# A list-scheduled encoder layer: new costs for the first loads and the shared port, sums moved behind the merges, one more Strassen pair

## The chip, the cores and the metric

The kernel runs on one core of one Trainium2 chip. The metric is the device time of one execution in microseconds. Engines are named as in the profile: PE (TensorE, matmuls and transposes), DVE (VectorE), ACT (ScalarE), POOL (GpSimd), SP (SyncE, which issues every DMA of this kernel).

## What is computed

One encoder layer is applied to a prompt of 512 tokens and to a sample of 1024 tokens, with the same weights and a model width of 1024. In the reference, shortened:

```python
h = rmsnorm(x, norm_g)
qa, ka, va, za, qb, kb, vb, zb, ga, gb = split(h @ w_in)
oa = (neighbourhood_attention(rmsnorm(qa), rmsnorm(ka), va, rpb_a) * silu(za)) @ w_o_a   # branch A, 8 heads
ob = (window_gqa_attention(rmsnorm(qb), rmsnorm(kb), vb, t5, sink) * silu(zb)) @ w_o_b   # branch B, 8 heads, 2 for k and v
merged = sigmoid(ga) * oa + sigmoid(gb) * ob
return x + merged @ w_out
```

All data is float32. The kernel multiplies at nearly that precision: every operand is split into a high part (`hi`, rounded by a copy on ACT) and a low part (`lo = x - hi`, a subtraction on DVE or POOL), and each product is three matmuls, hi*hi, hi*lo and lo*hi.

## The kernel before

**Who decides the order.** The program is written as a list of operations (`Flow.op`), each with the engines that may run it, a cost in ns for each, a priority (small is first), and the tiles it writes and reads. `Flow.run` is a list scheduler: it plays the operations through with those costs, gives every engine its next operation by priority, and writes the instructions in the order so found. On the chip each engine then works through its own fixed list and waits at semaphores; nothing is reordered there. SP's list of DMAs is made in the same way (`Flow.dma`: 470 ns on SP, then `nbytes / 360` ns of transfer), so a DMA that waits holds up every later one.

Three of the scheduler's rules matter here. A tag in `IN_TURN` gets its buffers in the order in which the program names the tiles. `port=True` marks an operation for which POOL and DVE exclude each other: while one of the two runs a marked operation, `barred` keeps marked operations off the other. Without a mark given, only operations that either engine may run are marked.

**Stages.** Prompt first (`attention_phase`, then `dense_phase`), then the sample, with the sample's normalisation hidden inside the prompt's phases.

- *Start*: x is loaded in tiles of 128 tokens (`norm_tile`). For the first tile ACT squares and sums (line 460), POOL makes 1/rms (464, 468), DVE multiplies by it and by the gains (line 520, four pieces of 256 columns; the gains row was spread over the partitions by PE at line 1629 and is copied to SBUF by ACT at line 1641), PE transposes (532), ACT and DVE split into `hh` and `hl` (537, 542). The first weights are split by ACT (line 602, `whi`) and POOL or DVE (line 607, `wlo`); `FIRST_POOL` sends the first one to POOL alone.
- *Attention*: for six groups (branch A 0 to 3, branch B 0 and 1) and each token tile, 24 matmuls of 384 columns (`project`, line 761), q and k normalised (785 to 816), transposed (`make_qk`, line 861) and split (882 to 901), scores (line 934), softmax (969 to 1010), transposes of the weights (1026), the product with v (1063). Branch B first gathers every 4th or 8th token column of `hh` and `hl` into `hb` (lines 662 and 664).
- *Dense*: projections z and the gates g, then the merges (for each of eight row blocks m: two products with w_o, times the gate, added, and split back into `hh`/`hl`, which are overwritten), then the projection with w_out. The last products are made in pairs of 128-row blocks, either classically (`pair_classic`: 4 banks of 24 matmuls for the sample) or by one step of Strassen's scheme (`pair_strassen`: 7 products of 12 matmuls). `CLASSIC_S` says how many z, g and w_out pairs of the sample are classic, `CLASSIC_P` the same for the prompt.

**The sums.** A Strassen pair needs four sums of blocks of the right-hand side. For w_out these are made by `sums`: for each k of 4, ten additions on DVE or POOL (line 1161, into three rotating `S` tiles) and four splits into `T` tiles (1167 on ACT, 1172 on DVE or POOL). The eight `T` buffers are held by the gated branch outputs until the merges' last products have read them. In the order before, all of this has priority 20, that of the first w_out pair; the merges have 12 to 19.

## Time and profile before

| what | value |
|---|---|
| three runs | 1144.78, 1145.87, 1147.69 us; median 1145.87 us |
| the profiled execution | 1146.52 us |
| its span, first to last instruction | 1144.7 us (1.8 us lie around it) |
| PE busy | 1133.8 us, 99% of the span |
| DVE, ACT, POOL busy | 854.4, 644.9, 308.3 us |
| merges of the sample end, w_out begins | 1059.7 us |

A PE matmul is recorded from its issue to its end and overlaps the next, so a mean of 389 ns is not what one costs: matmuls that follow each other start some 0.23 us apart at 512 columns. Idle time of PE is therefore looked for in the waits, not in the busy share.

### The profile page before, as it was taken

To read this page: it belongs to the slowest core of one execution; us is meant where nothing else is said; L and a number is where in the kernel's file an instruction comes from. 1 tells how busy PE (TensorE), PEld (TensorE's weight loads), DVE (VectorE), ACT (ScalarE), POOL (GpSimd) and SP (SyncE) were. 2 spreads that over 40 slices of the span, in tenths; PEclk is the share of its full clock that TensorE was granted. 3 is DMA by queue.
4 is the path that set the end of the run, shared out by engine and by line. 5 is a ranking of instruction groups with operands and counts; after the bars stand their busy time and mean duration, and the time that the engine had idled before them with its cause. 6 is when DMAs were issued, how large, how long until landed. Compare 5 with 4: busy or idle time off the path is not lost.

```text
span 1144.7 us, 18482 instructions
## 1 busy us (share of the span) xinstructions
PE 1133.8 (99%) x6139; PEld 985.8 (86%) x6139; DVE 854.4 (75%) x1975; ACT 644.9 (56%) x1467; POOL 308.3 (27%) x413
## 2 busy tenths in 40 slices
PE   8999999999999999999999999999999999999998
PEld 6999988888888899999999888888888888788887
DVE  5888798497765468887778888865878755497984
ACT  5777987544433346665678988865534434343320
POOL 3653433000010054343333445330222210132110
PEclk9999999999999999999999999999999999999999
DMA  7854543488786422121221213226657335573072
GB/s 253 273 158 141 181 113 102 115 264 266 232 277 199 165 72 67 25 70 32 71 61 50 56 37 93 56 66 214 218 148 211 129 111 159 200 238 121 29 223 90
DMA packets 124705, 159.86 MB, mean 140 GB/s; under 512 B 28297, under 2 KB 66961, under 8 KB 124610
## 3 DMA queue, kind: packets, MB, share of 16 engines
q1 hardware_dynamic: 124610, 158.69, 45.4%
q8 instruction: 48, 0.79, 0.3%
q14 instruction: 47, 0.39, 0.1%
HBM read 121.93 MB, written 41.44 MB: 143 GB/s over the span
## 4 chain that ended last, share of the span: by engine, by line
PE 94%; DVE 2%; DMA 2%; ACT 1%; POOL 1%; issue 0%; SPq 0%; ACTq 0%; POOLq 0%
PE p L761 25%; PE x L1285 9%; PE x L1286 9%; PE x L1284 9%; PE x L1063 5%; PE x L1026 5%; PE x L934 4%; PE p L1284 4%; PE p L1285 4%; PE d L1284 4%; PE p L1286 4%; PE d L1286 4%; PE d L1285 4%; PE x L861 2%; DMA ot<-u_d 1%; DMA w<-in_w_att_dram 1%
## 5 line engine op out<-in xcount | busy, mean ns | idle before, releaser
L761 PE MATMUL p<-whi,hh 128*128 128x384 f32 x384 | 133.4, 348 | 0.0
L761 PE MATMUL p<-wlo,hh 128*128 128x384 f32 x384 | 133.1, 347 | 0.0
L761 PE MATMUL p<-whi,hl 128*128 128x384 f32 x384 | 132.4, 345 | 0.0
L978 ACT ACTIVATE sb<-sb,mx 128x384 f32<-128x384 f32 (+1 forms) x192 | 107.5, 563 | 22.4 <-DVE mx L969 22.2
L1167 ACT ACTIVATE whi<-raw 128x512 fp32r<-128x512 f32 (+1 forms) x140 | 81.1, 590 | 52.6 <-PE x L1285 26.2
L761 PE MATMUL p<-whi,hb 128*128 128x384 f32 x384 | 107.5, 347 | 0.0
L1172 POOL TENSOR_TENSOR wlo<-raw,whi 128x512 fp32r<-128x512 f32 (+1 forms) x29 | 40.9, 1413 | 242.4 <-ACT whi L1167 130.4
L1284 PE MATMUL x<-hh,whi 128*128 128x512 f32 x264 | 102.7, 389 | 0.0
L1285 PE MATMUL x<-hl,whi 128*128 128x512 f32 x264 | 102.7, 389 | 0.0
L1286 PE MATMUL x<-hh,wlo 128*128 128x512 f32 x264 | 102.7, 389 | 0.0
L1037 DVE TENSOR_TENSOR pp<-x,pp 128x512 fp32r<-128x512 f32 (+1 forms) x136 | 82.6, 638 | 18.9 <-ACT pp L1032 17.8
L1172 DVE TENSOR_TENSOR wlo<-raw,whi 128x512 fp32r<-128x512 f32 (+1 forms) x111 | 70.1, 645 | 30.5 <-ACT whi L1167 30.2
L1285 PE MATMUL x<-T,whi 128*128 128x512 f32 x224 | 87.5, 390 | 0.3 <-DVE T L1172 0.2
L1286 PE MATMUL x<-T,wlo 128*128 128x512 f32 x224 | 87.2, 389 | 0.0
L1284 PE MATMUL x<-T,whi 128*128 128x512 f32 x224 | 87.1, 389 | 0.0
L1032 ACT ACTIVATE pp<-x 128x512 fp32r<-128x512 f32 (+1 forms) x136 | 70.9, 560 | 22.8 <-PE x L1026 21.8
L799 POOL TENSOR_TENSOR rs_r<-rs_v,mhalf 128x4 f32<-128x4 f32 (+1 forms) x72 | 81.7, 1134 | 5.7
L1063 PE MATMUL x<-pp,v 128*128 128x256 f32 (+1 forms) x368 | 77.8, 324 | 0.8 <-DVE pp L1037 0.8
L792 POOL TENSOR_SCALAR rs_v<-ss 128x4 f32<-128x4 f32 (+1 forms) x72 | 26.2, 364 | 187.3 <-DVE ss L785 184.6
L761 PEld LDWEIGHTS p<-whi,hl 128*128 128x128 f32 x384 | 73.0, 190 | 1.3 <-issue 1.0
L761 PEld LDWEIGHTS p<-wlo,hh 128*128 128x128 f32 x384 | 73.0, 190 | 1.0 <-issue 0.5
L761 PEld LDWEIGHTS p<-whi,hh 128*128 128x128 f32 x384 | 73.0, 190 | 0.9 <-issue 0.5
(351 smaller groups left out, 2985.5 us busy)
## 6 DMA issues: line engine op xcount, KB each, us to landing
raw<-in_w_g_dram SPq DMA_DIRECT2D x76, 256.0 KB
w<-in_w_att_dram SPq DMA_DIRECT2D x46, 384.0 KB
ot<-o_d SPq DMA_DIRECT2D x36, 256.0 KB
g_d<-C SPq DMA_DIRECT2D x34, 256.0 KB
raw<-in_w_z_dram SPq DMA_DIRECT2D x32, 256.0 KB
raw<-in_w_out_dram SPq DMA_DIRECT2D x32, 256.0 KB
C<-g_d SPq DMA_DIRECT2D x24, 256.0 KB
out_dram<-C SPq DMA_DIRECT2D x23, 256.0 KB
```

Of the source, the lines that this page charges most:

```text
L761: pe.matmul(ps.t[:, :GW], part[u](k), mv.t[:, c], start=k == 0 and m == 0, stop=k == KC - 1 and m == 2,)
L799: lambda e: nc.gpsimd.tensor_tensor(r.t[:, :nn], rv.t[:, :nn], mhalf[:, :nn], op=ALU.pow),
L978: act.activation(sb.t[:, :width], sb.t[:, :width], AF.Exp, bias=mx.t[:, i : i + 1], scale=-1.0, accum_out=sm.t[:, i : i + 1],)
L1026: pe.transpose(pt.t[:, u * P : (u + 1) * P], sbs[i].t[:, c * P : (c + 1) * P], ident)
L1032: lambda e, pt=pt, pp=pp, nn=nn: act.activation(pp.t[:, 0, :nn], pt.t[:, :nn], AF.Copy),
L1037: lambda e, pt=pt, pp=pp, nn=nn: dve.tensor_tensor(pp.t[:, 1, :nn], pt.t[:, :nn], pp.t[:, 0, :nn].bitcast(F32), op=ALU.subtract),
L1063: pe.matmul(out(), v.t[:, vs], mv(), start=first, stop=last)
L1167: (("act", ACT_(n)),), lambda e: act.activation(hi(), src(), AF.Copy), prio,
L1172: lambda e: engines[e].tensor_tensor(lo(), src(), hi().bitcast(F32), op=ALU.subtract), prio,
L1284: pe.matmul(out, hi.t[:, cs], mh(), start=first and k == 0, stop=False)
L1285: pe.matmul(out, hi.t[:, cs], ml(), start=False, stop=False)
L1286: pe.matmul(out, lo.t[:, cs], mh(), start=False, stop=last and k == len(ws) - 1)
```

## The change

- `dma`: transfers with a scheduled priority under -2, the first loads, are counted at 230 bytes per ns, not 360; the scheduler counts PE at 1.85 times its cost while its own clock is under 13000 ns.
- `att_weights`: the low part is marked `port=True` for every choice of engines, the one on POOL alone included.
- Costs: `make_qk`'s two DVE operations 105 ns less each, branch B's bias copy on ACT 76 ns more, the gather into `hb` on ACT 1000 ns, before 960.
- `hb` joins `IN_TURN`.
- `sums` for w_out takes a priority for each k (19.2 to 19.5, right behind the merges). For k = 0, 1, 2 the sums are stored to DRAM (`to_d`, 12 stores of 256 KB); later they are loaded back into `U` tiles (12 loads) and split from there at priority 20. For k = 3 they are split from `S` as before. The splits are now in the order in which Strassen uses them (j = 1, 2, 0, 3).
- `CLASSIC_S` ends in 1, not 2: one of the two classic w_out pairs of the sample becomes a Strassen pair.
- `SEED`, `SPREAD`, `SPAN`: with `SPREAD = 0` they shift no priority.

```diff
-CLASSIC_S = (1, 0, 2)
+CLASSIC_S = (1, 0, 1)
+SEED, SPREAD, SPAN, COLD = 0, 0, 1, 13000
+EARLY_RATE = 230
...
-    IN_TURN = {"whi", "wlo", "w32", "T", "S", "raw", "U", "C", "ot"}
+    IN_TURN = {"whi", "wlo", "w32", "T", "S", "raw", "U", "C", "ot", "hb"}
...
-        return self.op((("sp", 470),), lambda e: emit(), prio, lag=nbytes / 360, **kw)
+        return self.op((("sp", 470),), lambda e: emit(), prio, lag=nbytes / (EARLY_RATE if prio < -2 else 360), **kw)
...
-                        ns = dict(o.choice)[e]
+                        ns = dict(o.choice)[e] * (1.85 if e == "pe" and now < COLD and o.prio > -20.5 else 1)
...
-            tuple((e, {"pool": POOL_, "dve": DVE_}[e](n)) for e in engs), emit, prio, new=[lo], use=[hi], hold=[st], after=[a],
+            tuple((e, {"pool": POOL_, "dve": DVE_}[e](n)) for e in engs), emit, prio, new=[lo], use=[hi], hold=[st], after=[a], port=True,
...
-                    f.op((("act", ACT_(GW)),), emit, prio, new=first, use=[raw], into=[nb_t])
+                    f.op((("act", ACT_(GW) + 76),), emit, prio, new=first, use=[raw], into=[nb_t])
...
-                            (("act", 960), ("dve", DVE_(512))),
+                            (("act", 1000), ("dve", DVE_(512))),
...
-                (("dve", DVE_(P) + 165),),
+                (("dve", DVE_(P) + 60),),
...
-                (("dve", DVE_(n) + 165),),
+                (("dve", DVE_(n) + 60),),
...
-        def sums(prio, done):
+        def sums(split_prio, done, prios=None):
...
+                prio = prios[k] if prios else split_prio
...
                 for j in (0, 2, 1, 3):
-                    vh, vl = tv[j]
-                    ops[j, k] = split(
-                        lambda vh=vh, k=k: vh.t[:, k], lambda vl=vl, k=k: vl.t[:, k], lambda v=t[j]: v.t[:, :sn], sn, prio,
-                        (vh, k == 0), (vl, k == 0), [t[j]],
+                    if prios and k < 3:
+                        away.append((j, k, dma(
+                            lambda j=j, k=k, v=t[j]: nc.sync.dma_start(to_d[j, k], v.t[:, :sn]), 512 * sn, prio, use=[t[j]]
+                        )))
+                    else:
+                        away.append((j, k, t[j]))
+            for j, k, v in sorted(away, key=lambda a: ((1, 2, 0, 3).index(a[0]), a[1])) if prios else away:
+                vh, vl = tv[j]
+                if prios and k < 3:
+                    o, v = v, tile_("U", 4)
+                    dma(
+                        lambda j=j, k=k, v=v: nc.sync.dma_start(v.t[:, :sn], to_d[j, k]), 512 * sn, split_prio, new=[v],
+                        after=[o],
                     )
+                ops[j, k] = split(
+                    lambda vh=vh, k=k: vh.t[:, k], lambda vl=vl, k=k: vl.t[:, k], lambda v=v: v.t[:, :sn], sn, split_prio,
+                    (vh, j not in firsts), (vl, j not in firsts), [v],
+                )
+                firsts[j] = True
...
-        mov_h, mov_t = blocks(m_ops, nh), sums(20, m_ops) if o_classic < 4 else None
+        mov_h, mov_t = blocks(m_ops, nh), sums(20, m_ops, [19.2 + 0.1 * k for k in range(4)]) if o_classic < 4 else None
```

The prompt's w_out pairs are all classic, so `sums` with priorities is met in the sample alone. Counted over the whole program, PE has 12 matmuls of 512 columns less (6124 for 6136), SP 24 DMAs more, and DVE, ACT and POOL 5, 7 and 10 instructions more. The line numbers of the changed kernel are 4 larger up to the attention phase and 5 to 21 larger behind it (520 becomes 524, 607 becomes 611, 1161 becomes 1166, 1172 becomes 1177).

**The start, DVE.** `xt` is the first token tile, `x` a PSUM bank, `w_123` and `w_125` the second weight load, `bias` the tile that holds the third and fourth. Before:

```order
L520 SCALAR_TENSOR_TENSOR xt<-xt,nr,x 128x256 x2
L607 TENSOR_TENSOR wlo<-w_123,whi 128x768
L520 SCALAR_TENSOR_TENSOR xt<-xt,nr,x 128x256 x2
L542 TENSOR_TENSOR hl<-x,hh 128x2x128 x3
L520 SCALAR_TENSOR_TENSOR xt<-xt,nr,rb 128x512
L607 TENSOR_TENSOR wlo<-bias,whi 128x768
L542 TENSOR_TENSOR hl<-x,hh 128x2x128
```

Now:

```order
L524 SCALAR_TENSOR_TENSOR xt<-xt,nr,x 128x256 x4
L546 TENSOR_TENSOR hl<-x,hh 128x2x128 x2
L611 TENSOR_TENSOR wlo<-w_125,whi 128x768
L546 TENSOR_TENSOR hl<-x,hh 128x2x128 x2
L524 SCALAR_TENSOR_TENSOR xt<-xt,nr,rb 128x512
L611 TENSOR_TENSOR wlo<-bias,whi 128x768
L524 SCALAR_TENSOR_TENSOR xt<-xt,nr,rb 128x512
```

The low part of the second weights stood between the two halves of the first tile's multiplication; all four pieces now come first, and that low part stands behind two `hl` splits.

**The start, ACT.** `junk` is the square and sum of a token tile, the second one that of tile 1. Before:

```order
L460 ACTIVATE junk,ns<-xt 128x1024
L602 ACTIVATE whi<-w_121 128x768
L602 ACTIVATE whi<-w_123 128x768
L1641 ACTIVATE rb<-x 128x512
L460 ACTIVATE junk,ns<-xt 128x1024
L537 ACTIVATE hh<-x 128x2x128 x3
L602 ACTIVATE whi<-bias 128x768
```

Now:

```order
L464 ACTIVATE junk,ns<-xt 128x1024
L606 ACTIVATE whi<-w_123 128x768
L1662 ACTIVATE rb<-x 128x512
L606 ACTIVATE whi<-w_125 128x768
L541 ACTIVATE hh<-x 128x2x128 x2
L1662 ACTIVATE rb<-x 128x512
L541 ACTIVATE hh<-x 128x2x128 x2
L464 ACTIVATE junk,ns<-xt 128x1024
```

Tile 1's square stood ahead of tile 0's splits into `hh`; it now stands behind all four.

**The w_out projection of the sample, DVE.** Buffer numbers are kept. `hl_3331` and `hl_3377` are the low part of the merged activations, `d_`, `p_` and `x_` PSUM banks, `raw_` loaded weights, `S_` sums (of weights or activations). Before, from the last splits of the sums to the first Strassen weights:

```order
L1172 TENSOR_TENSOR T_12820<-S_13005,T_12811 128x512
L1161 TENSOR_TENSOR S_13025<-S_13025,hl_3331 128x512
L1161 TENSOR_TENSOR C_12680<-x_12822,C_12680 128x512
L1161 TENSOR_TENSOR C_12716<-x_12868,C_12716 128x512
L1161 TENSOR_TENSOR C_12764<-x_12910,C_12764 128x512
L1161 TENSOR_TENSOR C_12813<-x_12951,C_12813 128x512
L1172 TENSOR_TENSOR wlo_13051<-raw_12726,whi_12893 128x512
L1172 TENSOR_TENSOR wlo_13057<-raw_12747,whi_12917 128x512
L1172 TENSOR_TENSOR wlo_13066<-raw_12826,whi_12973 128x512
L1161 TENSOR_TENSOR C_12860<-d_12992,C_12860 128x512
L1161 TENSOR_TENSOR S_13094<-raw_13044,raw_13059 128x512
L1161 TENSOR_TENSOR C_13064<-p_13012,C_13064 128x512
```

Now, from the last splits of the sums on:

```order
L1166 TENSOR_TENSOR S_13050<-raw_12696,raw_12768 128x512
L1177 TENSOR_TENSOR T_13042<-U_13010,T_13026 128x512
L1177 TENSOR_TENSOR T_13042<-U_13022,T_13026 128x512
L1177 TENSOR_TENSOR T_13042<-S_13031,T_13026 128x512
L1166 TENSOR_TENSOR C_12842<-x_12997,C_12842 128x512
L1166 TENSOR_TENSOR S_13082<-raw_12667,raw_12696 128x512
L1166 TENSOR_TENSOR C_12880<-C_12880,U_13076 128x512
L1177 TENSOR_TENSOR wlo_13024<-S_13070,whi_12974 128x512
L1177 TENSOR_TENSOR wlo_13102<-S_13082,whi_13091 128x512
L1177 TENSOR_TENSOR wlo_13111<-S_13050,whi_13099 128x256
L1177 TENSOR_TENSOR wlo_13102<-S_13050,whi_13091 128x256
L1177 TENSOR_TENSOR wlo_13111<-raw_12768,whi_13099 128x512
```

Before, the first of these posts, `C_12680<-x_12822`, came 44 rows behind the last merge bank's addition (`U_12666<-x_12793`), and on PE the first product with a sum stood 216 matmuls behind the merges' last: two classic pairs and two products of the first Strassen pair. Now it stands 120 matmuls behind: one classic pair and two products. The low part of that product's weights, `wlo_13024<-S_13070`, comes 39 rows behind `U_12683<-x_12822`, the last merge bank's addition, and right behind `C_12880<-C_12880,U_13076`, where `U_13076` is ACT's copy of the first Strassen product's bank, `d_13052`.

**The w_out projection of the sample, SP.** `C` tiles are loaded from x and stored as output, `to_d` holds the sums. Before, from the merges' last loads on:

```order
L1249 DMA raw_12647<-in_w_out_dram 128x512
L1563 DMA U_12666<-g_d1024_94 128x512
L1249 DMA raw_12672<-in_w_out_dram 128x512
L1443 DMA C_12680<-in_xt_s_dram 128x512
L1443 DMA C_12716<-in_xt_s_dram 128x512
L1249 DMA raw_12726<-in_w_out_dram 128x512
L1249 DMA raw_12747<-in_w_out_dram 128x512
L1443 DMA C_12764<-in_xt_s_dram 128x512
L1443 DMA C_12813<-in_xt_s_dram 128x512
```

Now, at the same place, behind the merges' last loads:

```order
L1238 DMA U_12788<-to_d1024_95 128x512
L1464 DMA C_12795<-in_xt_s_dram 128x512
L1229 DMA to_d1024_95<-S_12773 128x512
L1229 DMA to_d1024_95<-S_12780 128x512
L1464 DMA C_12842<-in_xt_s_dram 128x512
L1229 DMA to_d1024_95<-S_12807 128x512
L1229 DMA to_d1024_95<-S_12848 128x512
L1464 DMA C_12880<-in_xt_s_dram 128x512
L1238 DMA U_12892<-to_d1024_95 128x512
L1229 DMA to_d1024_95<-S_12878 128x512
L1238 DMA U_12904<-to_d1024_95 128x512
```

Stores of sums and loads of them now stand between the loads of x and of the weights.

More of the change, by code (lines that the diff above doesn't have):

```diff
@@ L169, in op @@
         o.key, o.outs, o.eng = len(self.ops), [], None
+        if self.slack != 1:
+            o.prio += SPREAD * (hash((SEED, o.key // SPAN)) % 1000 / 1000 - 0.5)
         o.port = {"dve", "pool"} <= {e for e, _ in choice} if port is None else port
@@ L1146, in dense_phase @@
         u_d = dpool.tile([8, P, nt], F32, tag=f"u_d{nt}", name=f"u_d{nt}")
+        to_d = dpool.tile([4, 4, P, sn], F32, tag=f"to_d{nt}", name=f"to_d{nt}")
         g_d = dpool.tile([2, 8, P, nt], F32, tag=f"g_d{nt}", name=f"g_d{nt}")
@@ L1183, in moving_sums @@
             return mov
-        def sums(prio, done):
+        def sums(split_prio, done, prios=None):
             tv = [tuple(f.value(tp, [P, 4, sn], F32R, "T", 8) for _ in range(2)) for _ in range(4)]
-            ops = {}
+            ops, away, firsts = {}, [], {}
             for k in range(4):
+                prio = prios[k] if prios else split_prio
                 blk = lambda a, kk, n: (lambda: a.t[:, kk, n * sn : (n + 1) * sn].bitcast(F32))
```

## The prediction

> **What bounds the kernel now.** I read the page's first part, then PE's waits, then stretches of the span, then the order of time where PE waits.
>
> ```profile
> span 1144.7 us, 18482 instructions
> PE 1133.8 (99%) x6139; PEld 985.8 (86%) x6139; DVE 854.4 (75%) x1975; ACT 644.9 (56%) x1467; POOL 308.3 (27%) x413
> ...
> PE 94%; DVE 2%; DMA 2%; ACT 1%; POOL 1%; issue 0%; SPq 0%; ACTq 0%; POOLq 0%
> ```
>
> PE is busy for 1133.8 of 1144.7 us and carries 94% of the chain that ended last. What PE can be spared is a matmul less or a wait less. All its waits for another engine or a DMA are these:
>
> ```profile
> PE x L1629 <- DMA rb<-in_norm_row_dram: 4.4, 1, 4.4
> PE x L861 <- DVE qk L816: 1.0, 2, 0.5
> PE x L532 <- DVE xt L520: 0.9, 1, 0.9
> PE x L1063 <- DVE pp L1037: 0.8, 2, 0.6
> PE x L1026 <- DVE sb L1010: 0.3, 1, 0.3
> PE x L1285 <- DVE T L1172: 0.2, 1, 0.2
> ```
>
> That is 7.6 us in all: 4.4 us until the gains row has landed, 0.9 us right behind it, and six waits of 2.3 us together over the other 1130 us. Most of the rest of the 10.9 us without PE is the end:
>
> ```profile
> 1141.35 0.28 PE L1286 MATMUL p<-hh,wlo 128*128 128x256 f32 x1
> 1141.66 0.42 DVE L1161 TENSOR_TENSOR C<-C,p 128x256 f32<-128x256 f32 x1 [0.96 <-PE p L1286]
> ```
>
> From the last matmul's end at 1141.63 to the end of the span there are 3.1 us, for an addition and a store; they stay, since the last product is again made in two halves of 256 columns. So all waits together are worth 2.3 us, the start a few. Next, what one matmul costs and how full the other engines are; each row has, by engine, busy us and instructions:
>
> ```profile
> 4.40:11.00 6.60, 5.67 (x17) 3.90 (x17) 2.86 (x6) 4.76 (x10) 2.92 (x5) 1.00 0.97 359
> 800.00:940.00 140.00, 140.00 (x619) 115.95 (x618) 105.16 (x161) 59.90 (x117) 28.95 (x19) 1.00 0.55 169
> 1016.00:1060.00 44.00, 44.00 (x196) 36.44 (x195) 35.27 (x51) 16.73 (x29) 11.59 (x8) 1.00 0.51 163
> 1060.00:1090.00 30.00, 30.00 (x134) 24.85 (x133) 29.97 (x49) 10.64 (x18) 3.23 (x3) 1.00 0.09 29
> 1090.00:1120.00 30.00, 30.00 (x134) 24.83 (x133) 24.48 (x38) 8.29 (x18) 5.53 (x5) 1.00 0.68 216
> ```
>
> From 800 to 940 us PE runs matmuls of 512 columns alone, 619 in 140 us, so one is 0.226 us, without a pause. DVE is full in one stretch: 29.97 of 30 us behind the merges, where the sums are made.
>
> **Fewer matmuls.** One w_out pair of the sample turns from classic (4 banks of 24 matmuls, 96) to Strassen (7 products of 12, 84). 12 x 0.226 = 2.7 us less, all on the path, because PE is gapless there. This term has no other side unless a wait takes its place.
>
> **The start.** These rows show the first tile before:
>
> ```profile
> 1.53 0.82 SPq L600 DMA_DIRECT2D w<-in_w_att_dram  x2
> 4.42 3.75 PE L1629 MATMUL x<-rb,one 1*128 1x256 f32 x8 [4.42 <-DMA rb<-in_norm_row_dram]
> 6.68 0.87 DVE L520 SCALAR_TENSOR_TENSOR xt<-xt,nr,x 128x256 f32<-128x256 f32 x2 [5.68 <-PE x L1629]
> 7.84 0.85 ACT L602 ACTIVATE whi<-w 128x768 fp32r<-128x768 f32 x1 [1.72 <-DMA w<-in_w_att_dram]
> 8.10 1.11 PE L532 MATMUL x<-ident,xt 128*128 128x128 f32 x4
> 8.72 0.96 DVE L607 TENSOR_TENSOR wlo<-w,whi 128x768 fp32r<-128x768 f32 x1 [1.17 <-ACT whi L602]
> 9.30 1.06 ACT L460 ACTIVATE junk<-xt 128x1024 bf16<-128x1024 f32 x1
> 9.60 0.86 DVE L520 SCALAR_TENSOR_TENSOR xt<-xt,nr,x 128x256 f32<-128x256 f32 x2
> 10.13 1.14 PE L532 MATMUL x<-ident,xt 128*128 128x128 f32 x4 [0.92 <-DVE xt L520]
> 10.35 0.91 ACT L537 ACTIVATE hh<-x 128x256 fp32r<-128x256 f32 x3
> 10.92 0.67 PE L761 MATMUL p<-whi,hh 128*128 128x384 f32 x1
> ```
>
> DVE multiplied two pieces, then waited 1.17 us for the second weights (landed only at 7.84) and split them until 9.68, and only then took pieces three and four. PE sat idle for 0.92 us before 10.13. ACT made tile 1's square from 9.30 to 10.45 ahead of `hh`, so the first projection matmul came at 10.92. Now pieces three and four follow at once. Their bank is done when the gains matmuls end, 4.42 + 3.75 = 8.17. Two pieces take 0.86, so 8.3 to 9.15. The last four transposes then follow PE's first four (8.10 + 1.11) and end near 9.9 to 10.1, at 0.21 us apart. ACT has the first `hh` after the gains copy (0.58, from 7.7) and the second weights (0.85), at 9.15 + 0.39 = 9.5. The first matmul starts near 9.9, 1.0 us sooner. The low part moved back (0.96, now from about 10.4) is needed by the eighth matmul, seven steps of 0.3 us on, so it is covered. Tile 1's square and norm come 1.6 us later; its transposes have also moved back on PE, behind 13 matmuls instead of 15 at a slow 0.32 each, near 14.2, and its first multiplied half is due near 13.8, so that cover is 0.4 us thin. Some of the gain is lost later, because DVE still sets the pace 20 us on:
>
> ```profile
> 30.31 0.41 DVE L816 TENSOR_TENSOR qk<-p,rs_r 128x256 f32<-128x256 f32 x1
> 30.87 0.41 PE L861 MATMUL x<-ident,qk 128*128 128x128 f32 x2 [0.50 <-DVE qk L816]
> ```
>
> PE waits 0.50 us there for tile 1's q and k. DVE's list up to that row is as long now as before (row 37, before 36), while PE arrives sooner, so this wait is what comes late next. Ends: all of the 1.0 us kept, or nothing. I take half, -0.5 us.
>
> **The sums behind the merges.** Before:
>
> ```profile
> 1059.71 0.39 PE L1284 MATMUL x<-hh,whi 128*128 128x512 f32 x1
> 1061.19 0.68 DVE L1161 TENSOR_TENSOR U<-x,U 128x512 f32<-128x512 f32 x1
> 1088.17 2.48 DVE L1161 TENSOR_TENSOR C<-x,C 128x512 f32<-128x512 f32 x4
> 1108.67 0.39 PE L1284 MATMUL x<-T,whi 128*128 128x512 f32 x1
> ```
>
> w_out begins at 1059.71. DVE took the last merge bank's addition at 1061.19, 1.5 us later, and needed 44 rows, until 1088.17, for the sums of three of the four k: 27.0 / 44 = 0.61 us a row. The first product with a sum began at 1108.67, 49 us behind the merges, so there were 20 us to spare. Now that product is due after 120 matmuls, 27.1 us, and it needs the first sum's four splits and its weights. The splits are early: the last of them comes 19 rows behind the addition, 1.5 + 19 x 0.61 = 13.1 us. One of them, 15 rows behind (10.7 us), reads the sum of k = 2 back from DRAM: finished two rows behind the addition, at 2.7 us, stored and loaded. I bound such a DMA by the last store (addition done at 1142.1, span over at 1144.7, 2.6 us) and the second w load (issued by 2.4 at the latest, or at 1.5, landed at 7.84 with the DMA engines 0.97 busy; up to 6.3 us). At 2.6 us it is back at 7.9, in time; the DMA share was 0.09 in this stretch, so I take that end. Weights come last: `wlo_13024` stands 39 rows behind the addition, 1.5 + 39 x 0.61 + 0.6 = 25.9 us. POOL adds to that, with 2.5 more operations of 512 columns beside those rows than before:
>
> ```profile
> 1059.04 1.68 POOL L1161 TENSOR_TENSOR S<-hh 128x512 f32<-128x512 f32 x1 [0.63 <-DVE T L1172]
> 1059.49 1.78 DVE L1172 TENSOR_TENSOR T<-S,T 128x512 fp32r<-128x512 f32 x1
> ```
>
> DVE's subtraction took 1.78 us, not 0.68, next to POOL's: 1.1 us more. So 2.5 x 1.1 = 2.75 us at most and 0 at least (when DVE is on PSUM operands or waits anyway); half is 1.4, which gives 27.3 us. It cannot be sooner than the first Strassen product's end (108 matmuls, 24.4) plus ACT's copy (0.6) and two rows (1.2), 26.2 us. The first matmul that reads it is the third of its product, at 27.1 + 0.45 = 27.6 us. So the wait is 0 to 1.1 us (25.9 + 2.75 = 28.7), and about 1.3 us more if DVE comes into this stretch as late again as the 1.5 us. I take +0.5 us. The later products are 2.7 us apart and their splits and weights 1.2 to 2.4, so the cover grows behind it. The 24 DMAs (6.3 MB) lie where the DMA share was 0.51 and 0.09, and nothing else waits for them. In the merges the additions have the lowest priority: DVE's list over the last four row blocks has 53 rows (51 instructions before in those 44 us) and POOL's 14 tensor operations (8): 1.2 to 7.8 us more, with 8.7 us of DVE free, so nothing.
>
> **Costs, `port` and `hb`.** They add no instruction; they reorder DVE, ACT and POOL in both attention phases. What this does to the waits of 0.2 to 0.6 us there (L861, L1063, L1026) the trace cannot show: between -2.3 us (all gone) and +2.3 (twice as many). Nothing favours a sign; I take 0. `hb` in turn can make ACT wait for its buffer; its readers were never waited for by PE, so nothing.
>
> **Sum.** -2.7 - 0.5 + 0.5 + 0 = -2.7 us. Against the profiled execution, 1146.52, that is 1143.8. The median of the three runs is 0.65 us lower, 1145.87, and the forecast on that footing is 1143.2 us, 0.24% less. 0.3%, or 3.4 us, is about what a measurement of this kernel can tell from no change.
>
> **Rivals.** *Full rate sooner.* Matmuls of 384 columns start 0.32 us apart until 16.3 and 0.17 behind it:
>
> ```profile
> 14.91 0.52 PE L761 MATMUL p<-whi,hh 128*128 128x384 f32 x1
> 15.23 0.52 PE L761 MATMUL p<-wlo,hh 128*128 128x384 f32 x1
> 17.15 0.33 PE L761 MATMUL p<-wlo,hh 128*128 128x384 f32 x1
> 17.33 0.33 PE L761 MATMUL p<-whi,hl 128*128 128x384 f32 x1
> ```
>
> Granted clock in the rows above is 1.00, so only the spacing shows it. The rate rose 6.1 us after the pause that ended at 10.13. With that pause gone, work is unbroken from 4.42; if 6.1 us of it suffice, the rate rises at 10.5 and not at 15.2 (16.2 less the 1.0 us), and each us is worth 1 - 0.17 / 0.32 = 0.47: 2.2 us, giving 1141.0. Against it: 4.8 us of work before the pause had not raised it. The Trainium skill (TensorE: Matmul & The Clock Gate, Part 1) says the clock rises after a busy window of some 3.4 us, which runs free of the program, so that the number of slow matmuls varies from run to run; the spacing agrees with a slow start, and by that rule the gain would come in some runs and not in others.
>
> *The weights come late.* DVE comes out of the merges 3.0 us late, not 1.5, and every POOL operation costs its 1.1: `wlo_13024` at 30.2 us, a wait of 2.6, so -2.7 - 0.5 + 2.6 = -0.6, 1145.3. For it: both engines have more to do there; against it: the free 8.7 us.
>
> *Slower: the sums come back late from DRAM.* DVE's list holds the split of the returned sum 15 rows behind the addition, and the weights 24 rows behind that. A DMA of d us returns it at 2.7 + 2d; what goes over 10.7 us moves all that follows, and PE's 0.5 us wait grows by as much. At 6.3 us, the load's upper end, that is 4.6 us, and the change still comes out within the 0.3%, at 1147.8. It decides at d = 7.1: then the wait is 6.7 us and -2.7 - 0.5 + 6.7 = +3.5. At 8 us it would be 1151.2. For it: SP's list puts stores of output and loads that wait for a free tile between these DMAs; against it: the DMA share of 0.09.
>
> **Chances.** As summed 0.55 (own range 1141.5 to 1145, by the start's and the waits' ends); full rate sooner 0.13; weights late 0.18; slower by the sums' return 0.06; more waits in attention, 1144.5 to 1146, 0.08. Faster by over 0.3% (below 1142.4) are the clock case and a half of the first, 0.13 + 0.27 = 0.40; slower is 0.06 and a little of the last case, 0.07; between them 0.53. The range, 1139.8 to 1147.2, reaches from the clock case with all of the start kept (-2.7 - 1.0 - 2.2) to the late weights with most of a doubled set of waits (-0.6 + 1.9).
>
> **What would show it.** The first L761 matmul near 9.9, no DVE wait for `whi` ahead of it; 12 matmuls less; w_out shorter by 2.7 us; a PE wait of at most 1 us at L1307 for `wlo`, near 1086; PE's waits of 0.2 to 0.6 us again 2 us in all. Wrong it would be by a PE wait of over 2 us behind the merges, or by new waits in attention.

## The result, and the profile after

The changed kernel takes 1157.8 us (median of five runs, 1155.7 to 1161.8), the kernel before 1145.9: a ratio of 1.0101, 95% interval 1.0068 to 1.0134. It is 11.9 us slower where 2.7 us less were forecast. The profiled execution is the slowest of the five, 1161.8 us, so sizes are taken from medians below and places from the trace.

The page after, first PE's busy time, then the first line of the chain that ended last:

```profile
span 1159.9 us, 18529 instructions
PE 1135.7 (98%) x6127; PEld 984.5 (85%) x6127; DVE 871.7 (75%) x1980; ACT 641.2 (55%) x1474; POOL 323.1 (28%) x423
...
PE 76%; DVE 6%; DMA 4%; issue 1%; POOL 1%; ACT 1%; SPq 0%; DVEq 0%; POOLq 0%
```

PE carried 94% of the chain that ended last and now carries 76%; DVE and the DMAs have taken the most of it over. PE's waits, with us in total, times and the longest:

```profile
PE x L865 <- DVE qk L820: 6.2, 6, 1.9
PE x L1650 <- DMA rb<-in_norm_row_dram: 4.6, 1, 4.6
PE p L1305 <- ACT whi L1172: 4.1, 1, 4.1
PE x L1030 <- DVE sb L1014: 2.4, 3, 1.4
PE p L1307 <- DVE wlo L1177: 1.5, 1, 1.5
PE x L1067 <- DVE pp L1041: 0.6, 2, 0.4
```

Before, the six waits behind the start came to 2.3 us. Now q and k alone (L865, L861 before) cost 6.2 us, the weights of the first product with a sum 4.1 + 1.5 us, and the attention weights' normalisation (L1030) 2.4.

The start did what was said of it. DVE multiplies the third and fourth piece as soon as the gains are there (0.65 us of waiting for PE, no wait for `whi`), and the first projection matmul comes at 9.86 us, 10.92 before; matmuls are 0.18 us apart from 11.2 us on:

```profile
8.35 0.87 DVE L524 SCALAR_TENSOR_TENSOR xt<-xt,nr,x 128x256 f32<-128x256 f32 x2 [0.65 <-PE x L1650]
9.86 0.67 PE L765 MATMUL p<-whi,hh 128*128 128x384 f32 x1
10.32 0.52 PE L765 MATMUL p<-wlo,hh 128*128 128x384 f32 x1
11.21 0.34 PE L765 MATMUL p<-wlo,hh 128*128 128x384 f32 x1
11.39 0.33 PE L765 MATMUL p<-whi,hl 128*128 128x384 f32 x1
```

To see where the gain went, the traces are compared at equal work: each of PE's matmuls is counted at the spacing that its shape has at full rate (0.174 us for 384 columns, 0.227 for 512), and the work done so far is taken from the time. What is left is lost time, in us:

| work done, us | before | after | w_out part alone | costs alone |
|---|---|---|---|---|
| 20 (30 us into the span) | 11.5 | 10.2 | 10.1 | 10.1 |
| 380 (prompt done) | 22.2 | 29.3 | 22.0 | 25.0 |
| 920 (behind the sample's attention) | 47.0 | 56.7 | 48.4 | 49.2 |
| 1060 (w_out under way) | 47.9 | 65.8 | 57.7 | 50.2 |

The last two columns are the first two experiments. The total work fell from 1093.6 to 1090.9 us, the 2.7 us of twelve matmuls. The lost time grows in two places: in the prompt, and behind the merges.

**In the prompt.** One of the new waits, in order of time over ACT, POOL, DVE and PE:

```profile
49.73 0.85 ACT L606 ACTIVATE whi<-w 128x768 fp32r<-128x768 f32 x1 [1.31 <-DMA w<-in_w_att_dram]
50.65 1.86 POOL L611 TENSOR_TENSOR wlo<-w,whi 128x768 fp32r<-128x768 f32 x1 [2.55 <-ACT whi L606]
53.20 0.79 POOL L796 TENSOR_SCALAR rs_v<-ss 128x4 f32<-128x4 f32 x1
54.07 1.01 POOL L803 TENSOR_TENSOR rs_r<-rs_v,mhalf 128x4 f32<-128x4 f32 x1
55.12 0.42 DVE L820 TENSOR_TENSOR qk<-p,rs_r 128x256 f32<-128x256 f32 x1 [1.05 <-POOL rs_r L803]
55.69 0.41 PE L865 MATMUL x<-ident,qk 128*128 128x128 f32 x2 [1.74 <-DVE qk L820]
```

ACT stood 1.31 us for a load of weights, POOL's list holds the low part of those weights ahead of 1/rms of q and k, DVE waited 1.05 us for that, and PE 1.74 us for DVE. None of these instructions is new; their order in four lists is.

**Behind the merges.** w_out begins at 1069.58, right behind the merges' last product, and the first product with a sum stands 120 matmuls later, as counted:

```profile
1069.58 0.39 PE L1305 MATMUL x<-hh,whi 128*128 128x512 f32 x1
1075.52 0.68 DVE L1166 TENSOR_TENSOR U<-x,U 128x512 f32<-128x512 f32 x1
1098.04 0.63 ACT L1172 ACTIVATE T<-U 128x512 fp32r<-128x512 f32 x1 [2.26 <-DMA U<-to_d]
1098.70 1.10 DVE L1177 TENSOR_TENSOR T<-U,T 128x512 fp32r<-128x512 f32 x1 [0.80 <-ACT T L1172]
1101.01 0.80 PE L1305 MATMUL p<-T,whi 128*128 128x512 f32 x1 [4.07 <-ACT whi L1172]
1102.99 1.28 DVE L1177 TENSOR_TENSOR wlo<-S,whi 128x512 fp32r<-128x512 f32 x2
1103.73 0.80 PE L1307 MATMUL p<-T,wlo 128*128 128x512 f32 x1 [1.50 <-DVE wlo L1177]
```

DVE takes the last merge bank's addition 5.9 us behind the merges (1.5 before), waits for splits whose sums ACT waits for from DRAM (2.26 us at one place), and finishes the low part of the weights at 1103.68, 34.1 us behind the merges. PE would have come to it at 27.6.

The waits cost more than their length. Each row has the stretch, PE's busy time and matmuls, the granted clock, DMA share and GB/s:

```profile
416.00:418.00 2.00, 1.14 (x6) 0.82 0.01 5
418.00:420.00 2.00, 2.00 (x8) 0.50 0.37 98
1100.00:1104.00 4.00, 1.49 (x3) 0.50 0.45 123
1104.00:1107.00 3.00, 3.00 (x8) 0.54 0.80 243
1107.00:1110.00 3.00, 3.00 (x15) 1.00 0.73 238
```

Behind PE's pause of 4.07 us the granted clock is 0.50, and 0.54 in the next three us, which hold 8 matmuls where the three us behind them hold 15. The same follows a pause of 1.86 us at 415.

### The profile page after: what moved, and what is told of

Read it like the earlier page. It is cut to its first block, busy times and chain, and to the rows that moved or that the text cites. A ratio compares the mean times of both kernels' runs of the same rounds, so it can differ in the third digit from the quotient of the medians.

```text
span 1159.9 us, 18529 instructions
## 1 busy us (share of the span) xinstructions
PE 1135.7 (98%) x6127; PEld 984.5 (85%) x6127; DVE 871.7 (75%) x1980; ACT 641.2 (55%) x1474; POOL 323.1 (28%) x423
## 4 chain that ended last, share of the span: by engine, by line
PE 76%; DVE 6%; DMA 4%; issue 1%; POOL 1%; ACT 1%; SPq 0%; DVEq 0%; POOLq 0%
PE p L765 18%; PE x L1306 8%; PE x L1305 8%; PE x L1307 8%; PE x L1067 4%; PE x L1030 4%; PE x L938 4%; PE p L1307 4%; PE p L1305 4%; PE p L1306 3%; PE d L1305 3%; PE d L1307 3%; PE d L1306 3%; PE x L865 1%; DVE S L1166 1%
## 5 line engine op out<-in xcount | busy, mean ns | idle before, releaser
L1305 PE MATMUL x<-hh,whi 128*128 128x512 f32 (+1 forms) x268 | 103.5, 386 | 0.0
L1306 PE MATMUL x<-hl,whi 128*128 128x512 f32 (+1 forms) x268 | 103.4, 386 | 0.0
L1307 PE MATMUL x<-hh,wlo 128*128 128x512 f32 (+1 forms) x268 | 103.4, 386 | 0.0
L1177 POOL TENSOR_TENSOR wlo<-raw,whi 128x512 fp32r<-128x512 f32 (+1 forms) x35 | 49.4, 1419 | 159.9 <-ACT whi L1172 159.8
L1306 PE MATMUL x<-T,whi 128*128 128x512 f32 x228 | 89.0, 390 | 0.4 <-DVE T L1177 0.4
L1305 PE MATMUL x<-T,whi 128*128 128x512 f32 x228 | 88.8, 389 | 0.0
L803 POOL TENSOR_TENSOR rs_r<-rs_v,mhalf 128x4 f32<-128x4 f32 (+1 forms) x72 | 84.4, 1172 | 5.8
```

Of the source, the lines that this page charges most:

```text
L803: lambda e: nc.gpsimd.tensor_tensor(r.t[:, :nn], rv.t[:, :nn], mhalf[:, :nn], op=ALU.pow),
L1177: lambda e: engines[e].tensor_tensor(lo(), src(), hi().bitcast(F32), op=ALU.subtract), prio,
L1305: pe.matmul(out, hi.t[:, cs], mh(), start=first and k == 0, stop=False)
L1306: pe.matmul(out, hi.t[:, cs], ml(), start=False, stop=False)
L1307: pe.matmul(out, lo.t[:, cs], mh(), start=False, stop=last and k == len(ws) - 1)
```

## Experiments

Theory A: the loss is two parts that add, the w_out part and the new order of the attention phases. Ratios stand with their 95% intervals, times are medians of the runs, and the kernel before was between 1145.9 and 1146.4 beside them.

### The w_out part alone

```diff
-CLASSIC_S = (1, 0, 2)
+CLASSIC_S = (1, 0, 1)
...
-        mov_h, mov_t = blocks(m_ops, nh), sums(20, m_ops) if o_classic < 4 else None
+        mov_h, mov_t = blocks(m_ops, nh), sums(20, m_ops, [19.2 + 0.1 * k for k in range(4)]) if o_classic < 4 else None
```

> The kernel before with the w_out part of the change alone (one more Strassen pair, the sums behind the merges and over DRAM); the scheduling costs stay as they were. PE's list is the same as before up to the last 250 rows. Theory A (the loss of the changed kernel is made of two parts that add, this one and the order of the attention phases): 2.7 us of matmuls are gained, and some 8 us are lost behind the merges, as in the changed kernel's trace (waits of 4.1 and 1.5 us for the first product's weights, and 2 to 3 us at a halved granted clock behind them): 1151 us, 1.004 to 1.006 of before. Rival B (the loss comes with the chip's state or from earlier delays, and the w_out part itself is as I had predicted): 1143 to 1145 us and a wait under 1.5 us.

1152.6 us, 1.0054 (1.0038 to 1.0070). PE's waits, and the last 20 us of the merges with busy us and instructions of PE, weight loads, DVE, ACT and POOL:

```profile
PE p L1305 <- ACT whi L1172: 3.6, 1, 3.6
PE p L1307 <- DVE wlo L1177: 1.5, 1, 1.5
1041.60:1061.60 20.00, 20.00 (x90) 16.55 (x89) 19.85 (x25) 5.95 (x10) 11.68 (x9) 1.00 0.62 201
```

Theory A holds. The two waits (5.1 us) are there without any new order ahead of them, and the lost time grows by 7.8 us behind the merges: the waits and 2.6 us of slow matmuls. DVE is busy for 19.85 of the merges' last 20 us.

That is not the count of its operations. Over the merges' last 44 us DVE has 51 instructions here and 51 before, and is busy for 40.82 us where it was 35.27; POOL has 15 for 8, and is busy for 22.59 us where it was 11.29. In the last 20 us eight of DVE's operations of 512 columns took 1.07 to 1.78 us and not 0.68, each of them overlapping an operation of POOL; with no sums moved (next experiment) two did.

### One more Strassen pair and nothing else

```diff
-CLASSIC_S = (1, 0, 2)
+CLASSIC_S = (1, 0, 1)
```

> The kernel before with CLASSIC_S = (1, 0, 1) and nothing else: the sums stay at priority 20 and go straight from S to T. The first product with a sum is due 120 matmuls (27.1 us) behind the merges, and its weights stand 53 rows behind the last merge addition in DVE's list, about 1.5 + 53 x 0.61 = 33.8 us. If that list sets the pace (theory A), PE waits some 6 us and has 2 us more from a slower clock behind the wait: 1145.9 - 2.7 + 8 = 1151 us, so the detour over DRAM brought nothing. If the detour is what costs (rival C: sums straight from S come in time), 1143 to 1145.

1152.0 us, 1.0054 (1.0041 to 1.0067): the same as with the detour over DRAM.

```profile
1090.64 0.75 DVE L1177 TENSOR_TENSOR wlo<-raw,whi 128x256 fp32r<-128x256 f32 x2
1091.11 0.79 PE L1307 MATMUL p<-hh,wlo 128*128 128x512 f32 x1 [7.06 <-DVE wlo L1177]
1039.00:1059.00 20.00, 20.00 (x90) 16.56 (x89) 13.83 (x22) 7.34 (x14) 3.36 (x3) 1.00 0.35 113
```

DVE's list set the pace as expected (7.1 us against some 6), though PE stopped one product sooner than expected: at the low part of a loaded weight, row 50 of that list, done 32.1 us behind the merges and wanted at 25.1. By the time PE reached the product with a sum, its weights (row 53, 33.6 us) were done. Here DVE is busy for only 13.83 of the merges' last 20 us and comes out of them 1.5 us late, but has these 50 to 53 rows left.

### One and two of the sums moved

```diff
-                prio = prios[k] if prios else split_prio
+                prio = prios[k] if prios and k < len(prios) else split_prio
...
-                    if prios and k < 3:
+                    if prios and k < len(prios):
...
-sums(20, m_ops, [19.2 + 0.1 * k for k in range(4)])
+sums(20, m_ops, [19.2])
```

The second kernel has `[19.2, 19.3]` there; both change the w_out part alone.

> The w_out part alone, with only k = 0 of the sums moved into the merges and over DRAM; k = 1 to 3 stay behind them and go straight from S. Both ends cost PE 8 us behind the merges: all three moved (VectorE came 6.0 us late out of the merges and waited 3 us for loads of sums), and none moved (53 rows behind the last addition, which came 1.5 us late); in both the first product's weights were done 33.6 us behind the merges' end, wanted at 27.6. If VectorE's work is what limits (theory A), one moved k gives a middle: 43 rows x 0.61 = 26.2 behind an addition 2 to 4 us late, 29 to 31 us, a wait of 1.5 to 3 us, and if that is over 1.8 us, 2 us more from the halved clock: 1145 to 1148.5 us. If the detour's loads limit (rival), 8 loads for 24 free nearly all of it: 1143 to 1144.

> The w_out part alone, with k = 0 and k = 1 of the sums over DRAM and k = 2, 3 straight from S. PE's wait behind the merges was 7.1 us with none moved, 1.4 us with one, 5.1 us with three. If what is moved into the merges delays VectorE there (theory A: the last addition came 1.5 us late with none, 6.0 with three), two give a wait between one's and three's, 2 to 4 us, and where it is over 1.8 us some 2 us of slow matmuls behind it: 1147 to 1151 us. If the number of loads does not matter and three were only unlucky (rival), 1144 to 1146.

One: 1146.6 us, 1.0003 (0.9994 to 1.0012). Two: 1149.7 us, 1.0031 (1.0020 to 1.0043). PE's waits behind the merges, with one moved, then with two:

```profile
PE p L1305 <- ACT whi L1172: 1.0, 1, 1.0
PE p L1307 <- DVE wlo L1177: 0.4, 1, 0.4
```

```profile
PE p L1305 <- ACT whi L1172: 2.4, 1, 2.4
```

From the four traces, in us behind the merges' last product; the weights are those of the first product with a sum (with none moved, PE's wait was for those of row 50):

| sums moved | last addition | DVE rows to the weights | DVE idle | weights done | PE waited |
|---|---|---|---|---|---|
| none | 1.5 | 53 | 0.0 | 33.6 | 7.1 |
| k = 0 | 1.7 | 43 | 0.3 | 29.4 | 1.4 |
| k = 0, 1 | 4.4 | 39 | 0.4 | 30.9 | 2.4 |
| k = 0, 1, 2 | 6.0 | 39 | 2.8 | 33.6 | 5.1 |

The first ten additions just fit into DVE's free time in the merges (19.15 of the last 20 us busy, the last addition 0.2 us later). Ten more save four rows of 0.61 us behind the merges and bring DVE out of them 2.7 us later, so nothing is gained, and with three moved the loads come back too late as well. With one moved, 2.7 us of matmuls are saved, and 1.4 us of waits and some 0.5 of a slower restart are paid: no difference that can be measured.

### The scheduling costs alone

The changed kernel with `CLASSIC_S = (1, 0, 2)` and `sums(20, m_ops)`.

> The changed kernel without the w_out part (two classic pairs, sums at priority 20 and straight from S): only the scheduling costs, port and hb are changed. Theory A: the attention phases lose what they lose in the changed kernel's trace, some 10 us behind the kernel before at equal work: 1154 to 1157 us. Rival B: 1145 to 1147, with PE's waits 2 to 3 us in all.

1149.4 us, 1.0036 (1.0022 to 1.0051). Slower, but by 3.5 us and not by 8 to 11:

```profile
PE x L865 <- DVE qk L820: 2.2, 3, 1.2
PE x L1030 <- DVE sb L1014: 1.3, 2, 0.7
```

Its order is that of the changed kernel up to w_out, and still the trace of the one has lost 49.2 us at 920 us of work and that of the other 56.7. At 53 us PE waits 1.16 us here and 1.74 there, at 66 and 75 us not at all and 1.02 and 1.45. The changed kernel's profile is that of its slowest execution, so 3.5 us is the size of this part. Neither expectation had it: theory A had taken that slowest execution for the rule.

### The costs in pieces

The kernel before with `EARLY_RATE = 230`, `COLD = 13000` and `port=True`; with `EARLY_RATE` alone; with the port mark alone; and with the costs of `make_qk`, bias and `hb` alone.

> The kernel before with EARLY_RATE 230, COLD 13000 and port=True; make_qk, bias and hb costs stay. The first projection matmul comes near 9.9 us and the full matmul rate near 11 us, as in the changed kernel's trace. Theory A1 (the attention's new waits come from make_qk's lower DVE cost, which lets the scheduler put q and k late): this kernel keeps the 4 to 5 us of the start for the most part, 1141 to 1144 us. Theory A2 (they come from the reordered start, after which PE runs ahead of VectorE and the loads): it loses 5 to 8 us by 75 us as the changed kernel did, 1150 to 1156 us.

> The kernel before with EARLY_RATE = 230 and nothing else. It rewrites the start as in the changed kernel (all four pieces of the first tile first) and both attention phases behind it. Theory A2 (the reordered start costs the time): first projection matmul near 9.8 us, then PE's waits for q and k near 30 and 41 to 55 us of 2 to 4 us in all, and 1149 to 1153 us. Rival (the loss of the start kernel came from the PE factor or the port mark): within 2 us of before, 1144 to 1148.

> The kernel before with port=True on the weights' low part and nothing else. The order changes in the prompt's attention alone (PE's last 3835 rows are the same). If the mark does what it says, VectorE's operations beside POOL's first low part cost less and the prompt's waits for q and k fall: 1144 to 1146 us. Theory D (any rewriting of an order that was picked for the waits it has costs some): 1147 to 1150.

> The kernel before with the middle costs alone: make_qk's two VectorE operations 105 ns less, the bias copy 76 more, hb at 1000 and in turn; the start and w_out stay. All costs together lost 3.5 us (1149.4), the start's three alone 6.8 (1152.7). If the edits add (theory A), this one gains the difference: 1142 to 1144 us. If they don't, because each rewrites the whole order of the attention phases and the waits fall anew (theory D): anywhere from 1145 to 1151 us, with waits of 0.5 to 1.5 us for q and k at places that no single edit explains.

| on top of before | us | ratio (95%) |
|---|---|---|
| rate, PE factor and port | 1152.7 | 1.0057 (1.0042 to 1.0072) |
| rate alone | 1150.6 | 1.0044 (1.0032 to 1.0056) |
| port alone | 1157.8 | 1.0098 (1.0079 to 1.0117) |
| make_qk, bias, hb | 1150.8 | 1.0049 (1.0029 to 1.0069) |
| all of them (above) | 1149.4 | 1.0036 (1.0022 to 1.0051) |

They do not add: the middle costs alone should have gained and lost 4.7 us, and all together cost no more than any piece. The first two rows fell where theory A2 had put them, but the mark alone, which was to gain or to lose up to 4 us, lost 11.6. These two rows have the same lists but for one low part on DVE and one copy on ACT in the first 12 us, so the PE factor and the mark change nothing on top of the rate, and their 2 us between them show how far two sets of runs of one order lie apart. Without the rate the mark, which only tells the scheduler of an exclusion, draws another order and costs most, with waits of another kind. PE's waits with the mark alone:

```profile
PE x L1305 <- ACT hh L1172: 2.1, 1, 2.1
PE x L1674 <- POOL es L998: 1.4, 1, 1.4
PE x L1030 <- DVE sb L1014: 1.2, 2, 0.9
```

That speaks for theory D: an edit's content matters little, since each makes the scheduler draw a new order.

### Costs that say nothing new

```diff
-                (("dve", DVE_(P) + 165),),
+                (("dve", DVE_(P) + 164),),
...
-                (("dve", DVE_(n) + 165),),
+                (("dve", DVE_(n) + 164),),
```

> The kernel before with make_qk's two VectorE costs 1 ns lower (164 for 165) and nothing else: as a statement on the chip it says the same. PE's list is the same for its first 125 and last 2314 rows and differs between. Theory D (the order of before is one of many that the rules give, it has few waits, and any edit that makes the scheduler draw again loses some us): 1147 to 1152 us, with new waits of 0.5 to 1.5 us. Rival E (the edits' contents are wrong, a worse description of the chip; an order drawn with the same costs is as good): within 1.5 us of before, 1144.5 to 1147.5.

> As the last, with 5 ns less: a second draw of an order from costs that say nothing new; here both attention phases are drawn again. Theory D: again 1147 to 1155 us. Rival E: 1144.5 to 1147.5.

1 ns less: 1151.4 us, 1.0034 (1.0022 to 1.0046). 5 ns less: 1153.5 us, 1.0057 (1.0045 to 1.0070). First rows of 1 ns, then of 5 ns:

```profile
PE x L1030 <- DVE sb L1014: 1.2, 2, 0.9
PE x L865 <- DVE qk L820: 1.1, 3, 0.5
```

```profile
PE x L1030 <- DVE sb L1014: 3.0, 3, 1.4
PE x L865 <- DVE qk L820: 2.8, 4, 1.9
```

Rival E falls: 1 ns costs 5.0 us by the medians, 2.5 to 5.3 by the interval. At 380 us of work, five traces with the order of before have lost 20.3 to 22.2 us, and eight traces with six other orders 24.9 to 30.1. In the sample's attention the two kinds do not differ (24.6 to 26.4 us are lost between 380 and 920 us of work with the order of before, 22.6 to 27.4 with the others). The redrawn order costs in the prompt.

### What a pause of PE costs

```diff
+                    if pause and k == 0:
+                        for _ in range(pause):
+                            act.activation(pad_t, held.t[:, :120], AF.Copy)
+                        act.activation(ps.t[:, :120], pad_t, AF.Copy)
```

> The kernel before with eleven pauses of PE put into the sample's Strassen pairs: ahead of the second product of each pair ScalarE reads the first product's bank 1, 2, ... 10, 12 times (120 columns, some 0.2 us each) and writes the second's, and PE must wait for that. PE's list is unchanged, and the output is too. It measures what a pause costs by its length. Theory F (a pause of over about 1.8 us also halves the granted clock for some 3 to 4 us behind it): the short pauses cost their own length, those over 1.8 us also 1.9 to 2.6 us of matmuls started 0.43 us apart, with a granted clock of 0.5. Rival G (the halved clock came with the waits' places, where DMA and the other engines were busy, and not from the length): no slow matmuls behind any of them, or behind some short ones and not behind long ones. The pauses add some 1 + 0.2 x N us each, 11 x 2.2 = 24 us, and 6 x 2.2 = 13 us more by F: 1170 (G) or 1183 (F).

1188.3 us, 42 more: 27.9 us of pauses and 12.0 of slower spacing, by the trace. Three of the pauses, and stretches behind them (the fourth row of stretches follows a pause of 2.54 us, the last two take up the second again):

```profile
864.76 0.50 PE L1311 MATMUL x<-hh,whi 128*128 128x512 f32 x1 [1.97 <-ACT x L1309]
886.00 0.50 PE L1311 MATMUL p<-hh,whi 128*128 128x512 f32 x1 [1.87 <-ACT p L1309]
909.17 0.50 PE L1311 MATMUL p<-hh,whi 128*128 128x512 f32 x1 [2.24 <-ACT p L1309]
866.00:868.00 2.00, 2.00 (x10) 1.00 0.88 209
888.00:890.00 2.00, 2.00 (x6) 0.50 0.00 0
910.00:912.00 2.00, 2.00 (x10) 1.00 0.00 0
932.00:934.00 2.00, 2.00 (x6) 0.50 0.04 10
887.40:890.81 3.41, 3.41 (x10) 0.50 0.02 6
890.81:894.22 3.41, 3.41 (x16) 1.00 0.20 77
```

| pause, us | 0.67 | 0.97 | 1.33 | 1.87 | 1.97 | 2.24 | 2.54 | 2.84 | 3.14 | 4.05 | 6.34 |
|---|---|---|---|---|---|---|---|---|---|---|---|
| slower spacing behind it, us | 0.11 | 0.11 | 0.11 | 1.71 | 0.11 | 0.11 | 1.71 | 1.71 | 1.71 | 1.71 | 2.87 |
| of it in one step of 3.413 us, at most | 0.41 | 0.74 | 0.92 | 1.87 | 1.25 | 1.30 | 2.54 | 2.59 | 2.80 | 3.14 | 3.41 |

Rival G falls: the rows show a DMA share of 0.88 behind a pause that went free and of 0.00 behind one that did not. Theory F holds in that a halved clock follows some pauses, at the same price for nearly every length, but not by the length: 1.87 us paid it, 1.97 and 2.24 us did not.

What decides is in the trace. All changes of the granted clock in one trace lie whole steps of 3.413 us apart; here it falls at 887.40, rises at 890.81 and falls again at 931.77, 13 steps behind the first fall. A halved step loses half of 3.413, the 1.71 us of the table. A pause that lies across two steps is split by them: 2.24 us fell into 0.94 and 1.30 and went free, 1.87 us lay within one step. The table's last row gives the larger part. Counted over the 13 traces whose clock record has entries (that with one sum moved has none), the clock was full behind all 4302 steps in which PE was idle for up to 1.57 us, and halved behind all 19 with 1.82 us or more; a single step of 0.90 us, in a stretch already halved, was followed by another halved one. In the changed kernel's trace 1.74 us at 53 us went free, split into 1.53 and 0.21; 1.86 us at 415, in one step, did not; nor did 1.48 and 0.44 us together in one step with the middle costs alone.

The Trainium skill (TensorE: Matmul & The Clock Gate, Why this matters for your kernels) asks for no idle gap above some 3 us between bursts of matmuls; the runs put the edge lower, between 1.57 and 1.82 us within one step. Its Part 1 says that the window runs free of the program, and the steps agree: their first entry in the record stands anywhere from 11.10 to 16.15 us behind the start of the program.

## Why the prediction was wrong

**Fewer matmuls, -2.7 us.** Right: the work fell by that.

**The start, -0.5 us.** The events came as forecast. But the 1.0 us that they were measured against was largely one run's: in three other traces with PE's start order as before, the first projection matmul came at 10.2 to 10.6 us, not 10.92, since the second weights landed sooner. The rival of a full rate reached sooner came about, at 11.1 to 11.7 us in all four traces with the new start, where six with the old one have it at 12.0 to 16.3, of which the trace before was the latest. But nothing was left of either gain 30 us into the span, where the new start has lost 10.1 and 10.2 us and the old one, with the w_out part alone, 10.1. The cover that the prediction called 0.4 us thin did not hold: in the changed kernel's trace PE came to tile 1's transposes sooner, waited 0.58 us there, and 0.72 us at 30 us for q and k, where it had been 0.50.

**Costs, port and hb, 0 us.** This is the first step that failed. I bounded it by what the waits could lose and by the same amount upward, and wrote that nothing favours a sign. The trace had shown what does: PE waited 2.3 us in 1130, so a new order could gain 2.3 us at the most, and no row bounded what it could lose. Measured: +3.5 us for all the costs, and between +3.5 and +11.6 for six redrawn orders, of which none was faster.

**The sums, +0.5 us.** The second failed step. The place (first product with a sum, 120 matmuls behind the merges), the lists' row counts and the need at 27.6 us were right, and the weights were late, as the second rival had it; two sizes under it were wrong. DVE left the merges 6.0 us late, not 1.5 (3.0 in the rival): I set 1.2 to 7.8 us of new work in the merges' last 44 us against 8.7 us free and called that nothing. The new work measured 5.6 us and did fit into the 44, but the free time was not where the work came: the last 20 us were full (19.85 busy), and DVE was still full behind them. The loads from DRAM made DVE idle for 2.8 us; I had taken the quick end, 2.6 us for a DMA, and had named only in the rival, not in the sum, that they stand in SP's list behind stores and tiles that wait. That rival, priced at 4.6 us for the slow end, was a part of it. Together, 4.5 and 2.8 us, less some 1 us by which the rows behind the merges were quicker than set down, the weights came at 33.6 us, 6.3 later than the 27.3 forecast, and the waits were 5.1 us.

**The pause behind the pause, not in the sum.** The third: no term and no rival had a halved clock behind a wait, though the same trace showed matmuls of 0.32 us, not 0.17, at its start. It cost 2.6 us here, and 1.7 at 415 us in the trace after. (The prediction read a granted clock of 1.00 at the start; the trace's clock record has no entry before 16.15 us, and a stretch without an entry is printed as 1.00.)

In sum -2.7 + 5.1 + 2.6 + 3.5 = +8.5 us; the medians of the two parts alone give 6.7 + 3.5 = 10.2, and 11.9 (7.8 to 15.4) was measured. The range's lower end, 1139.8, is 0.2 us below its own terms, which changes nothing.

What stays open: which of the prompt's lists (loads, POOL, DVE) a new order runs into first. The chain at 50 us names a load and POOL, the port mark's waits name others, and taking the loads away was not tried. Nor do six draws tell how rare an order as good as that of before is.

## What to carry to other kernels

Where a list scheduler writes the program, an edit of its costs is a new draw of the whole order: bound its gain by the waits that are left in the trace and its loss by control edits that say nothing (1 ns here: some 4 to 5 us), and judge a cost model by several draws. Work moved ahead of a bottleneck helps only into free time of the engine that does it: look up that engine's busy share in the very stretch that receives the work, not over a longer one, count what its operations lose beside another engine's, and stop where it is full (ten additions fitted, thirty did not). Price a wait of PE with its clock: from some 1.8 us on, when it falls into one step of 3.413 us, its length and 1.7 us more; split over two steps up to 2.24 us went free here.

## What the runs showed of the hardware

The penalty for a pause was not expected to go by steps: the granted clock changed only at multiples of 3.413 us from its first entry, and what decided was how long PE had been idle in the step before, up to 1.57 us free, from 1.82 us not. Nine slow matmuls, 1.71 us, stood behind five pauses of very different length, and the granted clock shows them (0.50 in a stretch of 2 us). At the start of the program matmuls stood 0.32 us apart in stretches whose row prints 1.00, because the record has no entry there: its first one, at 16.15 us in the trace before and 11.10 in the one after, is the moment of the full rate. With the same order on PE this moment lay between 12.0 and 16.3 us in six traces.

Two executions of one order stood 7.5 us apart at 920 us of work. At one place the cause can be read: near 48 us ACT found a load of weights landed in the one and waited 1.31 us for it in the other. Whether loads make up the rest was not followed.
